# A two-layer hybrid backbone on one Trainium2 core: rooms for the two triangular solves, modulation weights by pairs, and other paces for the work run beside the matmuls

## The chip, the cores and the metric

The kernel runs on one core of a Trainium2 chip. The metric is the device time of one execution in microseconds (us); lower is better. Engines go by their names in the profile: PE is TensorE (matmuls and transposes; PEld its weight loads), DVE is VectorE, ACT is ScalarE, POOL is GpSimd, and SP issues most of the DMAs, from one queue in order. Each engine works through its own instructions in a fixed order and stops at the first one whose inputs are not there.

## The reference

The model has two layers on 256 latent tokens of width 2048, with 256 context tokens. Cut to what matters:

```python
# layer 0 (even): h = modulated latents, hc = modulated context
ka, va, kb, vb, a, b, qa, qb, za = split(h @ w_in)          # context: ka, va, kb, vb, a, b only
_, s_ctx = gdn_bidirectional(None, k_c, v_c, g_c, beta_c, zeros)   # recurrence over the context
o, _     = gdn_bidirectional(q, k, v, g, beta, s_ctx)              # recurrence over the latents
y_gdn = rmsnorm(o) * silu(za)
y_na  = neighbourhood_attention(qb, kb, vb, kb_ctx, vb_ctx, rpb)   # 8 heads
x = x + g1 * (concat(y_gdn, y_na) @ w_out)
x = x + g2 * swiglu(modulate(x, norm, sh2, sc2))
# layer 1 (odd): short convolution mixer, then the same kind of FFN
# per chunk of 64 tokens in gdn_bidirectional, for 8 heads and 2 directions:
t_inv = triangular_solve(eye + m, eye)     # m: 64 x 64, strictly lower
# and per layer: sh1, sc1, g1, sh2, sc2, g2 = split(silu(c) @ ada_w + ada_b)
```

All inputs are fp32.

## The kernel before, in words

**Matmuls.** Each product runs as three matmuls on values split into a high and a low part. A weight tile of 512 KB (`raw`) is loaded by SP, ScalarE copies its high part (`whi`, L176), VectorE subtracts to get the low part (`wlo`, L250), and TensorE multiplies with both. Three pairs of `whi`/`wlo` may stand ready at a time. TensorE needs a `wlo` from VectorE for every weight tile.

**Stages.** The input projection goes through its columns in the order KA, QA, VA (the recurrence's inputs), then KB and VB by halves (KB0, VB0, KB1, VB1: keys and values of the attention), QB0, QB1 (its queries) and ZA (the gate). The out projection follows in two halves (WO0, WO1), then the FFN of layer 0, and layer 1. Three kinds of side work run beside these stages, where the changed lines lie.

**1. The recurrence.** `chunk_matrices(1)` and `chunk_matrices(0)` prepare the context's and the latents' chunks: they build `nt` (the matrix m, L987), put aside its off-diagonal blocks (`n64`, `n32`), bring the 32 x 32 diagonal blocks into another layout by a store and eight gathers (`dl`, `lsol`), invert them in 31 pairs of VectorE instructions (L1029 product, L1031 subtract: "the solve") and store the result (`dz`). `inverses` joins blocks to 64 x 64 inverses, and `scan` goes over the chunks: each link is a fixed chain of matmul groups (L1123, L1132, L1143, L1165) with VectorE and ScalarE work between. `nt` and `lsol` share one room (tag "lsol"), and the context's `n64`/`n32` are written to DRAM (`nd64`, `nd32`) and read back. Which step of the stages calls which part is set by `plan`: `P_CH` for the latents' chunk, and the four numbers of `P_INV` for the inverses and scans; steps are counted from KB0 to QB1.

**2. The attention heads.** For each of eight heads `na_scores` loads a bias `bq` (L1307), adds a mask on VectorE (L1309), multiplies queries and keys (L1313, L1314) and takes the softmax (L1318 to L1322); `na_values` transposes and multiplies by the values (L1337).

**3. The modulation vectors of layer 0** (`ada_mixer`). Twelve blocks of 512 columns, each a sum over 16 weight tiles `araw` of 128 x 512: VectorE multiplies a tile by a scalar per partition and adds it to `acc` (L438). A block starts with a memset of `acc` (L430) and a DMA of its bias (L431), and closes with four matmuls (L445) that sum over partitions. `pump` takes a number of these steps per matmul step of the stage: `R_KB`, `R_QB`, `R_ZA` and `R_WO` are these paces. An L438 is tied behind the latest `wlo` at the place where it is written.

Within these bounds a scheduler at build time places the instructions of each engine.

At the hand-over from WO1 to the FFN a norm runs over the result: L1392 and L1393 add the projection to `xs`, L1411 scales a first half by the row norm (`rtmp`), L1447 the others (`xc`); TensorE transposes these, ScalarE modulates, and VectorE splits the FFN's inputs `fhi`, `flo` (L1459, L1465, L1466).

## Time and profile before

| | us |
|---|---|
| median of 3 runs | 2721.82 (2719.28 to 2724.71) |
| the profiled execution | 2726.88 |
| its span, first to last instruction | 2725.1 |
| TensorE busy in it | 2655.1 (97%) |
| VectorE busy in it | 1923.7 (71%) |
| ScalarE busy in it | 1279.2 (47%) |
| mean granted TensorE clock | 0.992 |

Durations and waits below come from the profiled execution. In its rows, "a <- b" says what an instruction writes and reads, or which releaser ended a wait; "x8" is a count. Where the stages lie in it, by TensorE's first and last matmul of each: KB0 from 337 us, VB0 from 387, KB1 from 438, VB1 from 493, QB0 and QB1 from 555 to 656, ZA from 661 to 738, the out projection from 743 to 874, and the FFN of layer 0 from 875. The context solve runs from 326 to 407 us, the latents' solve from 494 to 547.

### The profile page before, as it was taken

To read this page: it belongs to the slowest core of one execution; us is meant where nothing else is said; L and a number is where in the kernel's file an instruction comes from. 1 tells how busy PE (TensorE), PEld (TensorE's weight loads), DVE (VectorE), ACT (ScalarE), POOL (GpSimd) and SP (SyncE) were. 2 spreads that over 40 slices of the span, in tenths; PEclk is the share of its full clock that TensorE was granted. 3 is DMA by queue.
4 is the path that set the end of the run, shared out by engine and by line. 5 is a ranking of instruction groups with operands and counts; after the bars stand their busy time and mean duration, and the time that the engine had idled before them with its cause. 6 is when DMAs were issued, how large, how long until landed. Compare 5 with 4: busy or idle time off the path is not lost.

```text
span 2725.1 us, 37531 instructions
## 1 busy us (share of the span) xinstructions
PE 2655.1 (97%) x13775; PEld 2188.7 (80%) x13775; DVE 1923.7 (71%) x2652; ACT 1279.2 (47%) x1851; POOL 47.1 (2%) x73
## 2 busy tenths in 40 slices
...
GB/s 368 349 156 178 177 278 241 319 266 178 224 220 255 320 274 296 293 300 271 299 282 284 295 161 344 317 337 273 178 234 237 225 239 225 216 195 218 195 193 110
DMA packets 285124, 682.71 MB, mean 251 GB/s; under 512 B 56969, under 2 KB 98545, under 8 KB 283531
## 3 DMA queue, kind: packets, MB, share of 16 engines
...
q14 instruction: 77, 0.63, 0.1%
HBM read 658.16 MB, written 22.05 MB: 250 GB/s over the span
## 4 chain that ended last, share of the span: by engine, by line
PE 91%; DMA 3%; DVE 2%; ACT 2%; issue 1%; SPq 1%; DVEq 0%; ACTq 0%
PE mm L303 22%; PE mm L308 21%; PE mm L304 21%; PE mm L348 10%; PE mm L320 8%; PE sm L195 2%; PE sm L599 1%; PE gd L348 1%; DMA bq<-in_ev_rpb_dram 1%; DMA araw<-in_ada_w_dram 1%; PE sm L1337 1%; PE gd L1143 0%; PE gd L942 0%; DMA xn<-in_ctx_dram 0%; DVE wlo L250 0%
## 5 line engine op out<-in xcount | busy, mean ns | idle before, releaser
L250 DVE TENSOR_TENSOR wlo<-raw,whi 128x1024 fp32r<-128x1024 f32 x800 | 971.3, 1221 | 447.9 <-ACT whi L176 437.6
L176 ACT ACTIVATE whi<-raw 128x1024 fp32r<-128x1024 f32 x800 | 843.5, 1062 | 864.2 <-PE mm L308 636.2
L303 PE MATMUL mm<-whi,fhi 128*128 128x512 f32 x1232 | 482.3, 393 | 2.6 <-DVE fhi L1459 2.6
L304 PE MATMUL mm<-wlo,fhi 128*128 128x512 f32 x1232 | 479.8, 390 | 0.5 <-DVE wlo L250 0.5
L308 PE MATMUL mm<-whi,flo 128*128 128x512 f32 x1232 | 389.9, 390 | 0.0
L403 DVE SCALAR_TENSOR_TENSOR acc<-araw,cT,acc 128x1024 f32<-128x1024 f32 x224 | 286.5, 1279 | 37.6 <-DMA araw<-in_ada_w_dram 34.5
L303 PEld LDWEIGHTS mm<-whi,fhi 128*128 128x128 f32 x1232 | 231.6, 188 | 51.2 <-DVE fhi L1459 4.2
L308 PEld LDWEIGHTS mm<-whi,flo 128*128 128x128 f32 x1232 | 231.1, 188 | 48.4
L304 PEld LDWEIGHTS mm<-wlo,fhi 128*128 128x128 f32 x1232 | 231.5, 188 | 47.4 <-DVE wlo L250 0.9
L303 PE MATMUL mm<-whi,ahi 128*128 128x512 f32 x664 | 259.1, 390 | 0.0
L304 PE MATMUL mm<-wlo,ahi 128*128 128x512 f32 x664 | 258.3, 389 | 0.0
L348 PE MATMUL mm<-hB,whi 128*128 128x512 f32 (+1 forms) x840 | 235.3, 366 | 1.0 <-DVE hB L623 1.0
L308 PE MATMUL mm<-whi,alo 128*128 128x512 f32 x664 | 206.6, 389 | 0.0
L348 PEld LDWEIGHTS mm<-hB,whi 128*128 128x128 f32 x840 | 147.7, 189 | 24.3 <-DVE hB L623 2.2
L179 ACT ACTIVATE ahi<-prodT 128x256 fp32r<-128x256 f32 x176 | 73.1, 418 | 182.9 <-PE mm L304 178.1
L438 DVE SCALAR_TENSOR_TENSOR acc<-araw,cT,acc 128x512 f32<-128x512 f32 x192 | 142.4, 745 | 12.2 <-DMA araw<-in_ada_w_dram 10.9
L348 PE MATMUL mm<-hB,wlo 128*128 128x512 f32 (+1 forms) x420 | 149.5, 364 | 0.0
L308 PEld LDWEIGHTS mm<-whi,alo 128*128 128x128 f32 x664 | 124.6, 188 | 26.0
L303 PEld LDWEIGHTS mm<-whi,ahi 128*128 128x128 f32 x664 | 124.7, 188 | 25.7
L304 PEld LDWEIGHTS mm<-wlo,ahi 128*128 128x128 f32 x664 | 124.7, 188 | 25.5
L303 PE MATMUL mm<-whi,dhi 128*128 128x512 f32 x336 | 131.2, 393 | 1.2 <-DVE dhi L1459 1.2
L304 PE MATMUL mm<-wlo,dhi 128*128 128x512 f32 x336 | 130.8, 390 | 0.0
...
## 6 DMA issues: line engine op xcount, KB each, us to landing
...
raw<-in_ffn_w_down_dram SPq DMA_DIRECT2D x176, 512.0 KB
...
raw<-in_ev_w_in_dram SPq DMA_DIRECT2D x112, 512.0 KB
araw<-in_ada_w_dram SPq DMA_DIRECT2D x192, 256.0 KB
...
```

The lines of the kernel that those rows point to most:

```text
L176: ACT.activation(dst, src, AF.Copy)
L179: ACT.activation(hi, src, AF.Copy)
L195: return PE.transpose(dst, src, ident[:n, :n])
L250: last_lo[0] = DVE.tensor_tensor(lo, raw, hi, op=OP.subtract).ins
L303: PE.matmul(ps[ti][n], a, hi[:, n * 512:(n + 1) * 512], start=first, stop=False)
L304: ins = PE.matmul(ps[ti][n], a, lo[:, n * 512:(n + 1) * 512], start=False, stop=False).ins
L308: last_mm[0] = PE.matmul(ps[ti][n], b, hi[:, n * 512:(n + 1) * 512], start=False, stop=False).ins
L320: ins = PE.matmul(ps[ti][n], a(t), w[:, c_], start=False, stop=a is ll and hi is group[-1][0]).ins
L348: last_mm[0] = PE.matmul(o, wt, h_(slice(0, len(ws)), mv, k), start=i == 0 and g == 0 and j == 0, stop=i == len(ks) - 1 and g == len(group ...
L403: DVE.scalar_tensor_tensor(acc, raw, cT[:, k:k + 1], acc, op0=OP.mult, op1=OP.add)
L438: DVE.scalar_tensor_tensor(accs[n], raws.pop(i), cT[:, k:k + 1], accs[n], op0=OP.mult, op1=OP.add)
L599: ins = PE.matmul(pr[32 * j:32 * j + 32, :], cT2[:, g + j, :], raw[:, j].rearrange("p s n -> p (s n)"), start=g == 0, stop=g == KT - 4).ins
```

## The change

It has four parts.

- *Rooms.* The latents' chunk gets rooms of its own: `nt` and `lsol` lie in the two halves of `room`, the place that `state` takes later; `n32` and the solves' scratch lie in `half`. The context's off-diagonal blocks stay where they were built; the latents' `n32` alone goes through DRAM. Both quarters of the context's diagonal inverses are loaded at once.
- *Plan.* `P_CH` and the four numbers of `P_INV`.
- *Modulation weights.* One DMA brings two tiles (512 KB). The first tile of a block is a plain multiplication into `acc`, without memset and bias row; the bias is added to the closed sums as a column `bM`, which is transposed at the start together with the bias of the first two segments (`brow`, now 80 rows).
- *Paces.* `R_QB`, `R_KB`, `R_ZA`, `R_WO`.

```diff
@@ -41,16 +41,16 @@
 KH = 2
-P_CH = 2
-P_INV = (16, 22, 50, 56)
+P_CH = 1
+P_INV = (20, 26, 44, 50)
 AB = 6
...
 LATER = 2
-R_QB = 0.6
-R_KB = 1.6
-R_ZA = 2.0
-R_WO = 2.0
+R_QB = 1.5
+R_KB = 1.0
+R_ZA = 3.0
+R_WO = 1.6
 NST = 3
@@ -352,9 +352,14 @@
-    def ada_done(l, seg, kind, gamma, fs_, p):
-        if kind == "sc":
+    def ada_done(l, seg, kind, gamma, fs_, p, bias=None):
+        if bias is not None:
+            dst = scc[l, seg - 1] if kind == "sc" else (shc if kind == "sh" else gcol)[l, seg]
+            DVE.tensor_tensor(dst[:, fs_], p, bias, op=OP.add)
+            if kind == "sc":
+                DVE.scalar_tensor_tensor(dst[:, fs_], dst[:, fs_], 1.0, gamma[:, fs_], op0=OP.add, op1=OP.mult)
+        elif kind == "sc":
             DVE.scalar_tensor_tensor(scc[l, seg - 1][:, fs_], p, 1.0, gamma[:, fs_], op0=OP.add, op1=OP.mult)
@@ -426,16 +431,21 @@
             if not k:
-                acc = accs[n] = pool_.tile([128, 512], F32, name="acc", tag="acc", bufs=2)
-                DVE.memset(acc, 0.0)
-                SP.dma_start(acc[0:1, :], ada_b[0:1, c0:c0 + 512])
-            raws[i] = pool_.tile([128, 512], F32, name="araw", tag="araw", bufs=AB)
-            SP.dma_start(raws[i], wr[:, k, c0:c0 + 512])
+                accs[n] = pool_.tile([128, 512], F32, name="acc", tag="acc", bufs=2)
+            if k % 2:
+                return
+            raw = pool_.tile([128, 2, 512], F32, name="araw", tag="araw", bufs=AB // 2)
+            SP.dma_start(raw, wr[:, k:k + 2, c0:c0 + 512])
+            for j in range(2):
+                raws[i + j] = raw[:, j, :]
...
         def total(i):
...
             with tc.issue_after(last_lo[0]):
-                DVE.scalar_tensor_tensor(accs[n], raws.pop(i), cT[:, k:k + 1], accs[n], op0=OP.mult, op1=OP.add)
+                if k:
+                    DVE.scalar_tensor_tensor(accs[n], raws.pop(i), cT[:, k:k + 1], accs[n], op0=OP.mult, op1=OP.add)
+                else:
+                    DVE.tensor_scalar(accs[n], raws.pop(i), cT[:, 0:1], None, op0=OP.mult)
...
         def close(n):
@@ -443,11 +453,12 @@
                 PE.matmul(p[:, f:f + 1], acc[:, f * 128:(f + 1) * 128], ones[:, 0:1], start=True, stop=True)
-            ada_done(0, seg, kind, gamma, slice(b * 4, b * 4 + 4), p[:, 0:4])
+            m0 = (seg - 2) * 16 + b * 4
+            ada_done(0, seg, kind, gamma, slice(b * 4, b * 4 + 4), p[:, 0:4], bM[:, m0:m0 + 4])
             if kind == "row" and b == 3:
...
                 transpose(p[0:16, 0:128], gcol[0, seg])
-                g = pool_.tile([16, 128], F32, name="grow", tag="araw", bufs=AB)
+                g = pool_.tile([16, 128], F32, name="grow", tag="araw", bufs=AB // 2)
                 DVE.tensor_copy(g, p[0:16, 0:128])
@@ -457,7 +468,8 @@
                 total(i)
-                load(i + AHEAD)
+                if i:
+                    load(i + AHEAD - 2)
             if i >= KT + LAG - 1 and (i - LAG + 1) % KT == 0:
@@ -565,9 +577,9 @@
     ACT.dma_start(vrow[64:112, :], od_conv.rearrange("o t (k p) -> (o t k) p", p=128))
-    brow = sp.tile([32, 128], F32, name="brow")
+    brow = sp.tile([80, 128], F32, name="brow")
     bT = sp.tile([128, 32], F32, name="bT")
-    ACT.dma_start(brow, ada_b[0:1, 0:4096].rearrange("o (r p) -> (o r) p", p=128))
+    ACT.dma_start(brow, ada_b[0:1, 0:5 * D].rearrange("o (r p) -> (o r) p", p=128))
     ACT.dma_start(erow, ev_conv.rearrange("o t (k p) -> (o t k) p", p=128))
@@ -657,13 +669,15 @@
         p = smt()
-        transpose(p[:, 0:32], brow)
+        transpose(p[:, 0:80], brow)
         DVE.tensor_copy(bT, p[:, 0:32])
+        DVE.tensor_copy(bM, p[:, 32:80])
...
     gnb = epool.tile([128, 128], F32, name="gnb")
+    bM = epool.tile([128, 48], F32, name="bM")
@@ -871,7 +885,6 @@
     brest = epool.tile(gsh, F32, name="brest")
-    epool.tile([128, 48], F32, name="pad_e")
...
     def gates():
@@ -924,7 +937,8 @@
     flush()
-    state = gw.tile([128, 2, 8, 128], F32, name="state")
+    room = gw.tile([128, 2, 1024], F32, name="ntl", tag="state", bufs=1)
+    state = None
...
     def g4(name, tag, bufs=1):
@@ -954,6 +968,9 @@
+    half = []
+    nd32 = dram.tile([128, 16, 32], F32, name="nd32")
     def chunk_matrices(seq):
@@ -964,7 +981,7 @@
             n64 = lgo.tile([128, 1024], F32, name="n64", tag="o_t", bufs=2).rearrange("p (n c) -> p n c", n=16)
-            n32 = g4("n32", "vtok")[:, 0:512].rearrange("p (n c) -> p n c", n=16)
+            n32 = half[0][:, 0:512].rearrange("p (n c) -> p n c", n=16)
             dgs = lgo.tile([128, 1024], F32, name="dgs", tag="o_t", bufs=2)
@@ -977,7 +994,8 @@
                 tok = slice(ti * 128, ti * 128 + 128)
-                nt = gw.tile([128, 2, 4, 128], F32, name="nt", tag="lsol", bufs=1)
+                nt = (gw.tile([128, 2, 4, 128], F32, name="nt", tag="lsol", bufs=1) if seq else
+                      room[:, 0, :].rearrange("p (d i e) -> p d i e", d=2, i=4))
                 ems = [decay(d, t0 + ti, q) for d in range(2)]
@@ -1007,11 +1025,12 @@
-        lsol = g4("lsol", "lsol").rearrange("p (r c) -> p r c", r=32)
-        nd64 = dram.tile([128, 16, 64], F32, name="nd64", tag="nd64", bufs=2)
-        nd32 = dram.tile([128, 16, 32], F32, name="nd32", tag="nd32", bufs=2)
-        SP.dma_start(nd64, n64)
-        SP.dma_start(nd32, n32)
+        lsol = (g4("lsol", "lsol") if seq else room[:, 1, :]).rearrange("p (r c) -> p r c", r=32)
+        if seq:
+            half.append(g4("half", "vtok"))
+        else:
+            SP.dma_start(nd32, n32)
+            n32 = None
         dl = dram.tile([4, 32, 32, 32], F32, name="dl", tag="dl", bufs=2)
@@ -1022,7 +1041,7 @@
         POOL.memset(zsol.rearrange("p r c -> p (r c)")[:, ::33], 1.0)
-        sub_tmp = g2("sub_tmp").rearrange("p i e -> p (i e)")
+        sub_tmp = half[0][:, 512 + seq * 256:768 + seq * 256]
         for j in range(31):
@@ -1036,14 +1055,12 @@
                 SP.dma_start(dz[v, :, :, d].rearrange("b q t e -> (b q) t e"), src)
-        return nd64, nd32, dz
-    def load_offdiag(parts):
-        n64 = gw.tile([128, 16, 64], F32, name="n64", tag="n64", bufs=1)
+        return n64, n32, dz
+    def own_offdiag(n64):
         n32 = gw.tile([128, 16, 32], F32, name="n32", tag="n32", bufs=1)
-        SP.dma_start(n64, parts[0])
-        SP.dma_start(n32, parts[1])
+        SP.dma_start(n32, nd32)
         return n64, n32
...
     def load_diag(dz, q, tag="diag"):
@@ -1213,22 +1230,21 @@
     def own_chunks():
...
         own = chunk_matrices(0)
-        off = load_offdiag(parts)
-        diag = load_diag(parts[2], 0)
+        off = parts[:2]
+        diag = [load_diag(parts[2], q, ("diag", "kT")[q]) for q in range(2)]
...
     def first_inverse():
-        nonlocal diag
-        xdTs.append(inverses(off, diag, 0))
-        diag = load_diag(parts[2], 1)
+        xdTs.append(inverses(off, diag[0], 0))
...
     def second_inverse():
-        nonlocal off, diag
-        xdTs.append(inverses(off, diag, 1))
+        nonlocal off, diag, state
+        xdTs.append(inverses(off, diag[1], 1))
+        state = gw.tile([128, 2, 8, 128], F32, name="state", tag="state", bufs=1)
         for q in range(2):
...
         xdTs.clear()
-        off = load_offdiag(own)
-        diag = [load_diag(own[2], q, ("diag", "kT")[q]) for q in range(2)]
+        off = own_offdiag(own[0])
+        diag = [load_diag(own[2], q, ("diag", "n64")[q]) for q in range(2)]
...
     def first_own():
...
```

In the changed file L438 has become L446 (and L448 for a block's first tile), L445 L455, L984 to L1005 stand 18 lines lower (L987 is L1005), L1029 and L1031 are L1048 and L1050, the scan's groups stand 17 lines lower (L1123 is L1140, L1165 is L1182), and the heads and the norm 16 lines (L1313 is L1329, L1337 is L1353, L1411 is L1427, L1447 is L1463).

How the instructions move shows at three places. VectorE around the end of the context solve, before (L1032 copies the solve's result; L996 and L997 belong to the latents' chunk, and none of its rows of L987 stands above these):

```order
L1031 TENSOR_TENSOR zsol<-zsol,sub_tmp 128x2x30
L1029 TENSOR_TENSOR sub_tmp<-lsol,zsol 128x31
L1031 TENSOR_TENSOR zsol<-zsol,sub_tmp 128x31
L250 TENSOR_TENSOR wlo<-raw,whi 128x1024
L1032 COPY lsol<-zsol 128x1024
L438 SCALAR_TENSOR_TENSOR acc<-araw,cT,acc 128x512 x2
...
L987 SCALAR_TENSOR_TENSOR nt<-gd,beta,em 128x128 x8
L996 TENSOR_TENSOR em<-em,cs 128x512
L1002 STREAM_TRANSPOSE dgs<-nt 32x128 x4
```

and now, where `ntl` is the latents' `nt` and `half` the scratch:

```order
L1050 TENSOR_TENSOR zsol<-zsol,half 128x10x22
L1005 SCALAR_TENSOR_TENSOR ntl<-gd,beta,em 128x128 x3
L1048 TENSOR_TENSOR half<-lsol,zsol 128x207
L1005 SCALAR_TENSOR_TENSOR ntl<-gd,beta,em 128x128 x5
...
L1048 TENSOR_TENSOR half<-lsol,zsol 128x31
L1005 SCALAR_TENSOR_TENSOR ntl<-gd,beta,em 128x128 x8
...
L1051 COPY lsol<-zsol 128x1024
L1015 TENSOR_TENSOR AT<-gd,em 128x512 x2
...
L1005 SCALAR_TENSOR_TENSOR ntl<-gd,beta,em 128x128 x8
...
L1048 TENSOR_TENSOR half<-ntl,dgs 128x31
L1050 TENSOR_TENSOR dgs<-dgs,half 128x31
```

Three of the four groups of eight `ntl` rows stand inside the context solve, and the latents' solve (the last two rows) begins some 20 rows after the context's last link.

TensorE where the latents' scan ends and the out projection nears, before (L303 to L308 and L320 are the big matmuls; L195 are transposes, here of the softmax `s` and of `o_t`):

```order
L308 MATMUL mm<-whi,ylo 128x512 x2
L1123 MATMUL gd<-state,kT 128x128 x4
L1132 MATMUL gd<-state,qT 128x128 x4
L1143 MATMUL gd<-R,xdT 128x128 x4
L1165 MATMUL gd<-vn,AT 128x128 x4
...
L1313 MATMUL gd<-kb,qb 128x512
L1314 MATMUL gd<-bq,cs 128x256
...
L195 MATMUL gd<-cs,s 128x128 x4
L195 MATMUL sm<-cs,s 128x128 x4
L1337 MATMUL gd<-PT,vb 128x256 x4
...
L1337 MATMUL sm<-PT,vb 128x256 x4
```

and now, at the last two heads:

```order
L308 MATMUL mm<-whi,hC 128x512 x2
...
L1329 MATMUL gd<-kb,qb 128x512
L1330 MATMUL gd<-bq,cs 128x256
L1329 MATMUL sm<-kb,qb 128x512
L1330 MATMUL sm<-bq,cs 128x256
L303 MATMUL mm<-whi,hC 128x512
L304 MATMUL mm<-wlo,hC 128x512
...
L195 MATMUL gd<-cs,s 128x128 x4
L303 MATMUL mm<-whi,hC 128x512
L195 MATMUL sm<-cs,s 128x128 x4
...
L1353 MATMUL gd<-PT,vb 128x256 x4
```

The scan's links ended earlier, and groups of ZA's big matmuls (`hC`) stand between the heads' groups.

VectorE in the norm at the hand-over from WO1 to the FFN, before:

```order
L438 SCALAR_TENSOR_TENSOR acc<-araw,cT,acc 128x512
L223 SCALAR_TENSOR_TENSOR nx0s<-nx0s,nx0v 128x1
L224 SCALAR_TENSOR_TENSOR nx0r<-nx0s,nx0r 128x1
L1411 TENSOR_SCALAR rtmp<-xs,nx0r 128x512
L1392 TENSOR_TENSOR rtmp<-mm,row 128x512
L1393 TENSOR_TENSOR xs<-rtmp,xs 128x512
L358 SCALAR_TENSOR_TENSOR sc_84<-sm,vecT 128x4
L1459 CAST fhi<-modt 128x128 x4
...
L250 TENSOR_TENSOR wlo<-raw,whi 128x1024
...
L1447 TENSOR_SCALAR xc<-xs,nx1r 128x512
```

and now:

```order
L446 SCALAR_TENSOR_TENSOR acc<-araw,cT,acc 128x512
L1427 TENSOR_SCALAR rtmp<-xs,nx0r 128x512
L1408 TENSOR_TENSOR rtmp<-mm,row 128x512
L446 SCALAR_TENSOR_TENSOR acc<-araw,cT,acc 128x512
L1409 TENSOR_TENSOR xs<-rtmp,xs 128x512
L446 SCALAR_TENSOR_TENSOR acc<-araw,cT,acc 128x512 x3
L1475 CAST fhi<-modt 128x128 x2
...
L446 SCALAR_TENSOR_TENSOR acc<-araw,cT,acc 128x512 x2
L1418 TENSOR_REDUCE ss_7475<-ssx 128x1
...
L1463 TENSOR_SCALAR xc<-xs,nx1r 128x512
```

The products of the last modulation block (L446), which closed ahead of the norm before, stand between the norm's instructions, 12 of them between L1427 and the first L1463, and a first tile and three more (not shown) just ahead of L1427, where two stood before.

## The prediction, made before the changed kernel ran

> **What bounds the kernel now.** I read the page's engine totals and chain first, then the busy time by stretch, then the waits of TensorE and of VectorE in the stretches where TensorE loses time.
>
> ```profile
> span 2725.1 us, 37531 instructions
> ...
> PE 2655.1 (97%) x13775; PEld 2188.7 (80%) x13775; DVE 1923.7 (71%) x2652; ACT 1279.2 (47%) x1851; POOL 47.1 (2%) x73
> ...
> PE 91%; DMA 3%; DVE 2%; ACT 2%; issue 1%; SPq 1%; DVEq 0%; ACTq 0%
> ```
>
> TensorE is busy for 97% of the span. The change removes no matmul, so it can only win time in which TensorE stands, or runs at a lower clock. 2725.1 − 2655.1 = 70 us is idle. The stretches that hold the edited work:
>
> ```profile
> core 0: us, PE busy (x) PEld busy (x) DVE busy (x) ACT busy (x) POOL busy (x), PEclk, DMA share, GB/s
> 430.00:440.00 10.00, 8.91 (x48) 7.64 (x47) 9.47 (x21) 4.02 (x9) 1.61 (x4) 0.94 1.01 368
> 440.00:490.00 50.00, 50.00 (x316) 42.28 (x315) 38.68 (x72) 15.04 (x27) 4.21 (x10) 0.98 0.71 233
> 490.00:510.00 20.00, 18.72 (x236) 14.80 (x236) 16.49 (x37) 5.88 (x9) 0.95 (x1) 1.00 0.94 312
> 560.00:590.00 30.00, 23.76 (x173) 23.36 (x172) 14.98 (x27) 8.44 (x14) 1.81 (x1) 0.89 0.80 218
> 620.00:660.00 40.00, 34.93 (x656) 30.20 (x643) 21.64 (x41) 17.98 (x35) 0.00 (x0) 0.96 0.66 183
> 730.00:790.00 60.00, 51.15 (x286) 42.92 (x285) 37.75 (x92) 38.51 (x100) 0.00 (x0) 0.94 0.43 147
> 860.00:890.00 30.00, 25.56 (x117) 20.70 (x115) 23.22 (x52) 13.40 (x31) 0.00 (x0) 0.89 0.39 131
> ```
>
> The first number after the comma is TensorE's busy time, and PEclk its granted clock. Idle time plus (1 − clock) × length gives what each stretch loses: 430–490: 1.09 + 0.6 + 1.0 = 2.7 us; 490–510: 1.3; 560–590: 6.2 + 3.3 = 9.5; 620–660: 5.1 + 1.6 = 6.7; 730–790: 8.9 + 3.6 = 12.5; 860–890: 4.4 + 3.3 = 7.7. In all that is 40 us. No edit reaches the rest of the idle time but by a trifle at the head. The low clock stands behind an idle stretch each time; it is a cost of the stall.
>
> TensorE's waits name the causes (engine, line, whom it waited for, total, times, longest):
>
> ```profile
> PE mm L348 <- DVE wlo L250: 4.4, 1, 4.4
> ...
> PE sm L1337 <- DVE PT L173: 4.4, 2, 3.7
> PE gd L1143 <- DMA vtok<-vd__151: 1.9, 1, 1.9
> ...
> PE gd L1337 <- ACT PT L171: 3.7, 1, 3.7
> PE gd L1123 <- DVE state L1156: 1.5, 1, 1.5
> PE sm L195 <- DVE s L1322: 1.5, 1, 1.5
> PE gd L1165 <- DVE o_t L1137: 1.1, 1, 1.1
> ...
> PE sm L445 <- DVE acc L438: 3.2, 1, 3.2
> ```
>
> The first three lie in 560–660, the next four in 730–790, the last at the hand-over from the out projection to the first FFN. VectorE's own waits, of 320–440 and of 560–680:
>
> ```profile
> DVE sub_tmp L1029 <- DMA lsol<-dl: 4.6, 1, 4.6
> DVE nt L987 <- DMA dz<-lsol: 4.4, 1, 4.4
> ...
> DVE bq L1309 <- DMA bq<-in_ev_rpb_dram: 32.5, 8, 7.4
> ```
>
> VectorE works in order. A wait for a bias tile bq holds every wlo behind it, and TensorE needs a wlo for each weight tile. One stall traced whole:
>
> ```profile
> 570.01 0.56 DVE L1309 TENSOR_TENSOR bq<-bq,cs 128x384 f32<-128x384 f32 x1 [7.33 <-DMA bq<-in_ev_rpb_dram]
> 570.48 1.22 DVE L250 TENSOR_TENSOR wlo<-raw,whi 128x1024 fp32r<-128x1024 f32 x1
> ...
> 571.76 0.39 PE L348 MATMUL mm<-hC,wlo 128*128 128x256 f32 x1 [4.36 <-DVE wlo L250]
> ```
>
> **The change, part by part.**
>
> *Own rooms for the latent solve.* The latent chunk's nt no longer waits for the context solve's stores: 4.4 us of VectorE. The order shows the whole latent chunk pulled ahead: three of its four groups of L1005 stand inside the context solve (before, all came after it), and its solve starts some 20 VectorE rows after the context's. The gathers of lsol still stand ahead of it, so I keep one wait like the 4.6 us there. TensorE lost 2.7 us in 430–490, and the nt wait is the cause of its 1.09. I take a gain of 1.7, from 0 (the gathers' wait takes its place) to 2.7. 490–510 I leave as it is.
>
> The gain proper comes later. In the order of after, the latent scan's links lie 10 to 20 big matmuls apart from QB0 to ZA, and heads 6 and 7 of the attention lie inside ZA. Before, two whole links (L1123 to L1165) and both heads stood on TensorE with no big matmul between. A link or head waits for an answer from VectorE or ScalarE; the four waits of 730–790 (1.1 to 3.7 us) are these answers. A group of six big matmuls lasts 1.4 us, by the spacing of 0.23 that eight of them show in a row:
>
> ```profile
> 863.82 0.39 PE L320 MATMUL mm<-wlo,yhi 128*128 128x512 f32 x1
> ...
> 865.41 0.39 PE L320 MATMUL mm<-whi,ylo 128*128 128x512 f32 x1
> ```
>
> so two groups cover an answer of 2.8 us, and ten to twenty matmuls (2.3 to 4.6 us) nearly all. Of the 12.5 us I leave 2 for the o_t transposes still next to WO0: gain 10.5, from 5 (a head's answer of 3.7 us outlasts its cover, and the clock drops once) to 12.5.
>
> *QB0 and QB1.* The three bq loads that cost 7.3, 4.0 and 2.7 us at 570–586 now stand close together behind one weight load, so one wait of 7 stays in place of 14. With more link work in QB0, TensorE takes about a third longer for each tile, so three split tiles cover more. Of 9.5 us I take 4.5 as gained (0 to 8). In 620–660 the 3.7 us wait is a head's answer, which now has matmuls behind it: 3.5 of 6.7 gained (0 to 5.5).
>
> *Paces.* The same 192 multiply-adds are pumped elsewhere. Prices:
>
> ```profile
> L438 DVE SCALAR_TENSOR_TENSOR acc<-araw,cT,acc 128x512 f32<-128x512 f32 x192 | 142.4, 745 | 12.2 <-DMA araw<-in_ada_w_dram 10.9
> L250 DVE TENSOR_TENSOR wlo<-raw,whi 128x1024 fp32r<-128x1024 f32 x112 | 135.4, 1218 | 32.7 <-ACT whi L176 32.2
> L430 DVE MEMSET acc<- 128x512 f32 x10 | 4.8, 485 | 0.6
> ...
> 590.00:730.00 140.00, 134.93 (x1278) 116.93 (x1277) 93.97 (x176) 61.35 (x130) 2.76 (x2) 0.99 0.73 220
> ...
>   DVE acc L438: 10.9, 13
> ```
>
> Between the wlo's of QB1 and the end of ZA the order counts 45 multiply-adds in place of 34: 11 × 0.745 = 8.2 us. With the heads and links that moved in, the operations at their own rows' durations add about 20 us. VectorE was busy for 94 us of the 140 in 590–730, and waited there for most of the later bq loads. 94 + 20 = 114, plus some 18 of bq waits, is 132 of 140: it fits, with hardly any slack, and VectorE's order is fixed. Late wlo's could cost TensorE 0 to 16 us (two or three stalls as that of 4.4, each with 1.6 us of low clock). I take 4, nearest to the single stall on record.
>
> The other move is at the hand-over. The last ada block of 16 now runs inside the norm chain: 12 multiply-adds between L1427 and the first xc (L1463), none there before, and four instead of two just ahead of L1427. That chain in before:
>
> ```profile
> 869.28 0.49 DVE L1411 TENSOR_SCALAR rtmp<-xs,nx0r 128x512 f32<-128x512 f32 x1
> ...
> 874.52 0.63 DVE L1459 CAST fhi<-modt 128x128 fp32r<-128x128 f32 x4 [3.36 <-PE mm L320]
> ...
> 879.39 0.49 DVE L1447 TENSOR_SCALAR xc<-xs,nx1r 128x512 f32<-128x512 f32 x1
> ...
> 880.82 0.60 PE L195 MATMUL sm<-cs,xc 128*128 128x128 f32 x4
> ...
> 882.23 0.50 PE L303 MATMUL mm<-whi,fhi 128*128 128x512 f32 x1 [0.81 <-DVE fhi L1459]
> ```
>
> 14 instructions more at 0.66 us (0.745 less the 0.09 by which an instruction starts before the one ahead ends, as 570.01 + 0.56 and 570.48 show) are 9.2 us, of which the idle 3.36 us takes 3.4: xc comes about 6 us later, and TensorE, which has only the first 24 FFN matmuls ahead of it, stands for it. The 3.2 us wait for the closing L445 goes, since the block now closes behind those matmuls; but rtmp, next in line, comes 1.3 us later than before, so half of that wait stays. I take a loss of 7: 6 + 1.3 for the two delays, less 1.8 of the old wait, and 1.5 us more at the low clock; from 2 (cover by the next weight tiles) to 11 (both stalls, full low clock).
>
> A rule bears on that. The Trainium skill, "TensorE: Matmul & The Clock Gate", section "HAM oscillation — how this bites in real kernels", says that a wait which crosses the activity window drops TensorE to the half clock, and that the next work starts cold. The stretches above agree (0.89 in 860–890 beside 3.2 us of waiting); by the rule alone a 6 us wait would always bring a cold restart, and the hand-over would cost 8 rather than 7.
>
> *Paired loads and the bias column.* SP issues 96 araw and 12 bias loads fewer, at 0.33 us each by the row below; nothing on TensorE's path waits for them. Twelve memsets (12 × 0.485 = 5.8 us) go; the first product becomes a tensor_scalar (0.49 us for the same size, by the xc row) in place of a multiply-add. That relieves VectorE by 9 us over 700, hidden behind TensorE, and is in the balance above. Against it, pairs mean 3 rooms of two in place of 6, so a load can wait for two products. The 10.9 us that VectorE waited for araw may go or double; I count it at 0, ±1. At the head brow brings 80 rows in place of 32 ahead of erow on ScalarE's queue:
>
> ```profile
> L433 SPq DMA_DIRECT2D araw<-in_ada_w_dram x192: 327/328/2325, 140.2 to 860.6; - x192
> ...
> PE sm L195 <- DMA erow<-in_ev_conv_dram: 5.9, 1, 5.9
> ...
> L570 ACTq DMA_DIRECT2D brow<-in_ada_b_dram x1: 368/368/368, 3.0 to 3.0; - x1
> ```
>
> TensorE waits 5.9 us for erow; one more load as brow would be 0.4 us. I take 0.3 lost (0 to 0.5).
>
> **Sum.** 1.7 + 10.5 + 4.5 + 3.5 − 4 − 7 − 0.3 = 8.9 us gained. The profiled execution took 2726.88, 1.8 above its span and 5 above the median; it would come to 2718. By the median of the runs, 2721.82 − 8.9 = 2712.9.
>
> **Rivals.** *No change.* The heads' answers outlast their cover (10.5 becomes 6), VectorE costs 7, the hand-over 7, QB0/QB1 give 6: 1.7 + 6 + 6 − 7 − 7 − 0.3 = −0.6, about 2722. For it speaks that the two losses are in the order itself; against it, that 730–790 is the largest and its cause is plainly moved.
>
> *Slower: VectorE becomes the bound in QB1 and ZA.* The multiply-adds that R_QB 1.5 puts into QB1 share VectorE with bq waits, and in-order wlo's come late. It decides once VectorE's work and waits in 590–730 exceed TensorE's 140 us, so if the bq waits there stay above 26 instead of my 18 (32.5 stood in 560–680). Price 16, and QB0/QB1 give only 3 as the same waits bite there: 1.7 + 10.5 + 3 − 16 − 7 − 0.3 = −8, about 2730.
>
> *A larger gain.* The hand-over costs 2, since the next weight tiles stand ready, and VectorE 0: 1.7 + 12.5 + 6 + 4 − 2 − 0.3 = 22, about 2700. For it: three split tiles were full before 730; against it: the norm chain feeds all FFN matmuls.
>
> *The solves don't run at once.* The order shows the context solve's last link before the latent solve's first. Only the chunk overlaps; had the links not moved with it, gains of 1.7 and the losses would be left, 2731. The links did move, so I fold its small chance into the slower case.
>
> **Numbers.** Forecast (2706 to 2717) 0.38; no change 0.22; slower 0.20; larger gain 0.20. A difference of 0.2% (5.4 us) is about what a measurement of this kernel can tell from none. So faster 0.38 + 0.20 = 0.58, same 0.22, slower 0.20. The bounds summed would reach from 2695 to 2735; leaving out a tenth at each end gives 2700 to 2729. The likeliest case's own range is 2706 to 2717.
>
> **What would show it.** Right: no wait above 2 us on TensorE where ZA passes to WO0, L1353 there without a 3.7 us wait; a clock of 1.00 over it; the wait of L1005 for dz gone; at the hand-over a wait of 5 us or more for xc or fhi with L446 rows ahead of it on VectorE. Wrong: TensorE waits on wlo L250 of several us in QB1 and ZA with bq rows ahead (the slower case); no wait at the hand-over (the larger gain); bq waits above 30 us in all. If the context and latent links stand next to each other again, the first term was misread.

## The result, and the profile after

The changed kernel takes 2738.95 us, median of 4 runs (2734.23 to 2739.94), beside 2722.59 for the kernel before in the same comparison. The ratio is 1.0057, 95% interval 1.0042 to 1.0072: slower by 16 us, where 9 us of gain were forecast, and outside the range. The profiled execution took 2739.08 us, so it stands for the median; that of before took 2726.88, some 4 above its own.

The page of the changed kernel, first the totals and then the chain of work that ended last:

```profile
span 2737.3 us, 37225 instructions
...
PE 2656.9 (97%) x13775; PEld 2189.4 (80%) x13775; DVE 1918.1 (70%) x2645; ACT 1282.1 (47%) x1852; POOL 49.9 (2%) x73
...
PE 83%; DMA 7%; DVE 6%; ACT 1%; issue 1%; SPq 1%; POOL 0%; DVEq 0%; ACTq 0%
```

TensorE works as long as before (2655.1) on as many matmuls, and VectorE 5.6 us less. What grew is idle time, 70.0 to 80.4 us, and time at a low clock. TensorE's share of the chain fell from 91% to 83%; DMA and VectorE took it.

Busy time by stretch in the changed kernel (columns as in the prediction: length, TensorE busy, ..., PEclk). The stretches are KB1, QB, ZA, the 40 us from ZA's end, and the hand-over (14 us before the last matmul of the out projection to 26 us behind it); the same five in the kernel before follow:

```profile
447.00:511.00 64.00, 57.66 (x437) 47.19 (x436) 43.37 (x86) 16.82 (x28) 0.95 (x1) 0.95 0.72 220
568.00:686.00 118.00, 104.80 (x1194) 95.58 (x1193) 83.59 (x160) 46.66 (x105) 0.00 (x0) 0.96 0.81 246
686.00:768.00 82.00, 80.43 (x419) 66.31 (x417) 53.70 (x108) 43.90 (x103) 0.00 (x0) 1.00 0.45 135
768.00:808.00 40.00, 34.01 (x145) 27.11 (x144) 34.42 (x54) 18.22 (x20) 0.00 (x0) 0.87 1.02 405
864.00:904.00 40.00, 30.79 (x135) 24.55 (x134) 33.53 (x70) 15.70 (x32) 0.00 (x0) 0.83 0.56 172
```

```profile
436.00:493.00 57.00, 55.91 (x344) 47.27 (x344) 44.76 (x85) 19.18 (x36) 5.82 (x14) 0.97 0.72 235
555.00:656.00 101.00, 90.72 (x1072) 83.04 (x1073) 57.20 (x106) 41.82 (x85) 4.58 (x3) 0.95 0.79 229
656.00:738.00 82.00, 80.97 (x470) 69.22 (x467) 55.27 (x102) 35.82 (x80) 0.00 (x0) 1.00 0.62 193
738.00:778.00 40.00, 31.23 (x187) 25.84 (x186) 30.14 (x69) 28.08 (x76) 0.00 (x0) 0.99 0.58 197
860.00:900.00 40.00, 35.56 (x162) 28.97 (x161) 33.11 (x64) 23.40 (x51) 0.00 (x0) 0.91 0.46 153
```

Idle time plus (1 − clock) × length, as in the prediction, gives the loss of each stage; the last column is the forecast gain worked out there. PEclk has two digits, so a long stretch is good to half a us.

| stage | before | after | change | forecast |
|---|---|---|---|---|
| KB1 | 1.1 + 1.7 = 2.8 | 6.3 + 3.2 = 9.5 | 6.7 lost | 1.7 gained |
| QB | 10.3 + 5.1 = 15.4 | 13.2 + 4.7 = 17.9 | 2.5 lost | 8.0 gained |
| ZA | 1.0 | 1.6 | 0.6 lost | 4 lost |
| ZA's end | 8.8 + 0.4 = 9.2 | 6.0 + 5.2 = 11.2 | 2.0 lost | 10.5 gained |
| hand-over | 4.4 + 3.6 = 8.0 | 9.2 + 6.8 = 16.0 | 8.0 lost | 7 lost |

These make 19.8 us. VB1 gives 1.3 back, the rest of the out projection 2.5, and what follows takes 1.2 more: 17 in all. The spans of these two executions differ by less, 12.2 us (idle time 10.4 more, busy time 1.8), and the medians by 16.4. The sum is too high in part because idle time at a low clock counts twice in it (2.0 us of that at the hand-over, below). So the losses show where time goes, and do not add up to the kernel's time to better than some 5 us. Of the two losses that were forecast for these stages, the hand-over's came at its size and ZA's hardly; the three gains did not come at all.

TensorE's waits in these stretches of the changed kernel, KB1 first, then QB, ZA's end and the hand-over:

```profile
PE gd L1160 <- DMA vtok<-vd__152: 3.6, 1, 3.6
PE mm L348 <- DVE nst L173: 2.7, 2, 2.1
...
PE sm L1353 <- DVE PT L173: 4.6, 2, 2.3
PE sm L195 <- ACT s L1336: 2.4, 1, 2.4
PE gd L1109 <- issue: 1.8, 1, 1.8
...
PE mm L303 <- ACT whi L176: 4.8, 2, 2.6
PE mm L304 <- DVE wlo L250: 1.2, 1, 1.2
...
PE sm L195 <- DVE rtmp L1427: 4.3, 1, 4.3
PE sm L455 <- DVE acc L446: 2.6, 1, 2.6
PE mm L303 <- DVE fhi L1475: 1.7, 2, 0.9
```

**KB1.** The wait of nt for the solve's stores is gone, and so is TensorE's wait for nt. In its place the context scan, whose matmuls on vtok begin some 48 us earlier than before (490.1 and 538.1 us), waits for vtok. SP's queue and TensorE there:

```profile
477.59 1.22 SPq L1057 DMA_DIRECT2D dz<-dgs  x2
478.94 2.89 SPq L1057 DMA_DIRECT2D dz<-ntl  x2
481.88 1.23 SPq L963 DMA_DIRECT2D vtok<-vd__152  x1
...
490.06 2.05 PE L1160 MATMUL gd<-vtok,xdT 128*128 128x128 f32 x8 [3.60 <-DMA vtok<-vd__152]
```

`half`, the scratch of both solves, lies in the place of vtok. The latents' solve uses it to its last subtraction, at 477.0 us; then SP issues the four stores of the solve, and only then the load of vtok, which arrives 8 us later. The diff says so (`g4("half", "vtok")`). The 2.7 us of waits for nst, the copies of the stage's results, make up the rest of the 6.3 us idle here; what delays them was not traced.

**ZA's end.** The heads' answers are indeed covered: no wait for them is left there. But the out projection's first weights come late. SP's queue:

```profile
741.95 0.53 SPq L1344 DMA_DIRECT2D vb<-vb_d  x1
765.46 0.38 SPq L438 DMA_DIRECT2D araw<-in_ada_w_dram  x1
765.93 1.86 SPq L236 DMA_DIRECT2D raw<-in_ev_w_out_dram  x2
```

and what held it from 742 to 765 (SP's waits from 718 to 798 us: line, whom it waited for, total, times, longest):

```profile
SPq L438 <- DVE acc L446: 28.0, 6, 23.0
```

A load of modulation weights stood at the head of the queue for 23.0 us until a product (L446) freed its room, and the loads of the out projection stood behind it. TensorE ended ZA at 768.1; the first of these loads had been issued 2.2 us earlier.

**Hand-over.** VectorE's and TensorE's rows:

```profile
874.00 0.48 DVE L1427 TENSOR_SCALAR rtmp<-xs,nx0r 128x512 f32<-128x512 f32 x1
...
877.41 1.54 DVE L446 SCALAR_TENSOR_TENSOR acc<-araw,cT,acc 128x512 f32<-128x512 f32 x2 [0.40 <-DMA araw<-in_ada_w_dram]
...
888.72 0.49 DVE L1463 TENSOR_SCALAR xc<-xs,nx1r 128x512 f32<-128x512 f32 x1
```

```profile
874.63 1.09 PE L195 MATMUL sm<-cs,rtmp 128*128 128x128 f32 x4 [4.34 <-DVE rtmp L1427]
...
888.40 1.67 PE L455 MATMUL sm<-cs,acc 128*128 128x1 f32 x8 [2.64 <-DVE acc L446]
```

From rtmp to xc VectorE takes 14.7 us, where it took 10.1 (869.28 to 879.39): the products in between. TensorE stands for rtmp, and then at the closing sum (L455), just ahead of xc's transposes. Behind each of the two waits its clock is at half:

```profile
871.59:878.41 6.82, 3.65 (x10) 2.58 (x10) 6.39 (x15) 1.97 (x6) 0.00 (x0) 0.50 0.78 235
888.65:895.48 6.83, 6.02 (x21) 4.84 (x21) 5.93 (x14) 3.39 (x6) 0.00 (x0) 0.50 0.00 0
```

In these 13.7 us TensorE is idle for 4.0, half of which the loss of 16.0 counts twice; counted once it is 14.0.

### The profile page after: what moved, and what is told of

Same layout as the page of the kernel before. It is cut to its first block, busy times and chain, and to the rows that moved or that the text cites. A ratio compares the mean times of both kernels' runs of the same rounds, so it can differ in the third digit from the quotient of the medians.

```text
span 2737.3 us, 37225 instructions
## 1 busy us (share of the span) xinstructions
PE 2656.9 (97%) x13775; PEld 2189.4 (80%) x13775; DVE 1918.1 (70%) x2645; ACT 1282.1 (47%) x1852; POOL 49.9 (2%) x73
## 4 chain that ended last, share of the span: by engine, by line
PE 83%; DMA 7%; DVE 6%; ACT 1%; issue 1%; SPq 1%; POOL 0%; DVEq 0%; ACTq 0%
PE mm L303 20%; PE mm L304 20%; PE mm L308 20%; PE mm L348 9%; PE mm L320 7%; DMA araw<-in_ada_w_dram 3%; PE sm L195 2%; DVE wlo L250 1%; DMA bq<-in_ev_rpb_dram 1%; DVE acc L446 1%; PE sm L611 1%; PE gd L348 1%; DVE acc L408 1%; PE gd L956 1%; DMA raw<-in_ev_w_out_dram 1%
## 5 line engine op out<-in xcount | busy, mean ns | idle before, releaser
L303 PE MATMUL mm<-whi,fhi 128*128 128x512 f32 x1232 | 483.0, 394 | 3.0 <-DVE fhi L1475 3.0
L308 PE MATMUL mm<-whi,flo 128*128 128x512 f32 x1232 | 390.1, 390 | 0.0
L303 PEld LDWEIGHTS mm<-whi,fhi 128*128 128x128 f32 x1232 | 232.0, 188 | 51.9 <-DVE fhi L1475 4.8
L308 PEld LDWEIGHTS mm<-whi,flo 128*128 128x128 f32 x1232 | 231.1, 188 | 48.4
L303 PE MATMUL mm<-whi,ahi 128*128 128x512 f32 x664 | 259.0, 390 | 0.0
L308 PE MATMUL mm<-whi,alo 128*128 128x512 f32 x664 | 206.5, 389 | 0.0
L308 PEld LDWEIGHTS mm<-whi,alo 128*128 128x128 f32 x664 | 124.6, 188 | 25.9
L303 PEld LDWEIGHTS mm<-whi,ahi 128*128 128x128 f32 x664 | 124.6, 188 | 25.8
L446 DVE SCALAR_TENSOR_TENSOR acc<-araw,cT,acc 128x512 f32<-128x512 f32 x180 | 134.5, 747 | 9.8 <-DMA araw<-in_ada_w_dram 8.2
L303 PE MATMUL mm<-whi,dhi 128*128 128x512 f32 x336 | 131.1, 393 | 2.3 <-DVE u_t L1630 1.2
```

The costliest lines, as they stand in the source:

```text
L303: PE.matmul(ps[ti][n], a, hi[:, n * 512:(n + 1) * 512], start=first, stop=False)
L308: last_mm[0] = PE.matmul(ps[ti][n], b, hi[:, n * 512:(n + 1) * 512], start=False, stop=False).ins
L446: DVE.scalar_tensor_tensor(accs[n], raws.pop(i), cT[:, k:k + 1], accs[n], op0=OP.mult, op1=OP.add)
```

## The experiments

The theory after reading the trace: the paces decide. R_KB 1.0 takes products out of KB and VB, where VectorE has slack (busy 29 of the 60 us from 500 to 560 in the changed kernel), and leaves a backlog that stands in the norm at the hand-over and, on SP's queue, ahead of the out projection's weights. Rivals: the rooms, whose sharing holds up the context scan; and the paired loads, whose three rooms hold SP's queue.

Each kernel below was compared with the kernel before on the same chip. The losses are worked out as in the table above, from each kernel's profiled execution. That took from 8 us less (new rooms with R_KB 2.0; 6 less with the other scratch) to 5 us more than the kernel's median, so differences of a few us between the rows' losses need not stand in the medians. "Products" are those of the modulation blocks, counted between the wlo's of a stage in the kernel's order.

| kernel | median us | ratio to before (95%) | KB1 | VB1 | QB | ZA's end | hand-over |
|---|---|---|---|---|---|---|---|
| changed kernel | 2738.95 | 1.0057 (1.0042–1.0072) | 9.5 | 0 | 17.9 | 11.2 | 16.0 |
| changed, old paces | 2724.75 | 1.0014 (1.0004–1.0023) | 11.9 | 2.9 | 8.6 | 9.4 | 9.6 |
| before, new paces | 2734.72 | 1.0049 (1.0032–1.0066) | 6.7 | 0 | 17.7 | 11.2 | 20.5 |
| before, new rooms | 2721.75 | 1.0003 (0.9993–1.0013) | 8.0 | 1.5 | 7.9 | 9.1 | 9.0 |
| changed, single loads | 2743.66 | 1.0086 (1.0071–1.0101) | 5.6 | 0 | 18.0 | 1.6 | 25.8 |
| changed, R_KB 1.6 | 2726.12 | 1.0014 (1.0004–1.0025) | 11.8 | 4.8 | 17.8 | 8.1 | 1.5 |
| changed, R_KB 1.3 | 2724.44 | 1.0011 (1.0002–1.0021) | 9.2 | 0 | 17.7 | 6.9 | 1.4 |
| changed, late products left out | 2723.32 | 1.0003 (0.9994–1.0013) | 6.5 | 0 | 15.2 | 10.6 | 1.5 |
| changed, R_QB 0.6 | 2750.03 | 1.0097 (1.0079–1.0115) | 10.0 | 0 | 20.7 | 11.0 | 19.8, and 11 behind |
| changed, old paces, other scratch | 2729.37 | 1.0023 (1.0010–1.0036) | 8.6 | 2.2 | 14.9 | 0.8 | 8.5 |
| before, pairs | 2732.80 | 1.0038 (1.0023–1.0053) | 0 | 6.4 | 28.9 | 10.5 | 4.2 |
| before, new rooms and plan | 2721.59 | 0.9999 (0.9990–1.0008) | 11.6 | 1.0 | 8.9 | 11.3 | 6.5 |
| before, new rooms, R_KB 2.0 | 2736.20 | 1.0050 (1.0035–1.0065) | 9.4 | 14.5 | 5.7 | 10.6 | 1.4 |
| changed, old paces, R_KB 2.0 | 2738.69 | 1.0060 (1.0039–1.0081) | 15.9 | 9.8 | 9.0 | 15.9 | 1.4 |
| before, new rooms, R_QB 1.0 | 2718.22 | 0.9984 (0.9974–0.9994) | 12.1 | 1.0 | 14.9 | 8.6 | 1.5 |
| changed, single loads, R_KB 1.6 | 2724.58 | 1.0008 (0.9998–1.0017) | 9.8 | 2.4 | 15.0 | 9.1 | 1.5 |
| changed, loads from GpSimd | 2761.66 | 1.0150 (1.0129–1.0171) | 13.8 | 0 | 33.3 | 4.7 | 32.2 |
| the same, R_KB 1.3 | 2732.52 | 1.0039 (1.0020–1.0058) | 1.4 | 0 | 23.5 | 8.5 | 1.4 |

**Which of the three parts.** One part undone, or one part alone:

```diff
 # old paces (changed kernel), and the reverse in the kernel before
-R_QB, R_KB, R_ZA, R_WO = 1.5, 1.0, 3.0, 1.6
+R_QB, R_KB, R_ZA, R_WO = 0.6, 1.6, 2.0, 2.0
 # new rooms alone: only the hunks on room, half, nd32 and the diagonals
 # single loads: the modulation hunks of the diff taken back
```

> The changed kernel with the four old paces back (R_QB 0.6, R_KB 1.6, R_ZA 2, R_WO 2); rooms, plan and paired loads stay. Its order has no modulation product behind L1427 any more (the changed kernel has 12). If the paces are the cause (they take products out of KB and VB, where VectorE has slack, and leave a backlog that ends in the norm at the hand-over and ahead of the out projection's weight loads), it comes down by 14 to 22 us from 2739, to 2717 to 2725, and the stall at the hand-over falls from 16 us (idle and low clock in 860-900) to the 8 of before or less. If the rooms are the cause (the context scan's vtok and the evacuations of VB0 wait behind the latents' solve), it stays at 2731 or more, since that part is unchanged. If the paired loads are the cause, it stays at 2735 or more.

> The kernel before with the four new paces alone. If the paces are the cause: slower than before by 8 to 18 us (2731 to 2741), with a hand-over as in the changed kernel (15 products stand behind the norm's first scaling in its order). If rooms or paired loads are the cause: within 4 us of before.

> The kernel before with the new rooms alone (old plan, old paces, single loads). If the paces are the cause of the whole loss: within 5 us of before, to the faster side (2717 to 2723), since the latents' chunk no longer waits for the stores. If the rooms are the cause (scratch of both solves in the place of vtok until the latents' solve has ended): slower by 6 to 12 us (2729 to 2735), with waits of TensorE on vtok and nst in 440-500.

> The changed kernel with single modulation loads, memsets and bias rows back; rooms, plan and new paces stay. If pairs are the cause (three rooms of two tiles hold SP's queue ahead of the out projection's weights): faster than 2739 by 8 us or more. If the paces are the cause: no faster, rather slower by 2 to 8 us (2739 to 2747), since 26 products instead of 12 stand behind the norm's first scaling.

The old paces bring the changed kernel from 1.0057 to 1.0014; the new paces alone cost the kernel before 1.0049. The rooms alone cost nothing that can be told. Single loads make it worse, as there are then 26 products in the norm instead of 12 (hand-over 25.8). So the paces are the main cause, and neither rooms nor pairs are. The table shows where: the hand-over and QB. The parts do not simply add up, though. With new paces and single loads, the rooms and their plan cost something after all (1.0086 beside 1.0049): there are 26 products in the norm instead of 15. And KB1's loss rises with the rooms alone (8.0, from 2.8) as well as with the paces alone (6.7). One expectation missed: the old paces brought the hand-over to 9.6, not to 8 or less.

**Which pace.** R_KB and R_QB undone singly, in the changed kernel:

```diff
-R_KB = 1.0
+R_KB = 1.6        # after_kb16
-R_QB = 1.5
+R_QB = 0.6        # after_qb06
```

> The changed kernel with R_KB back at 1.6 alone; R_QB 1.5, R_ZA 3 and R_WO 1.6 stay. In its order KB0 to VB1 hold 92 products instead of 58, and none stands behind the norm's first scaling. If the low R_KB is the cause (products taken out of stages with slack come back as a backlog at the hand-over), the hand-over falls from 16 us to 8 or less and the time to 2722 to 2731. If the high R_QB is the cause (25 products in QB1 beside the waits for bq), the time stays at 2733 or more, with QB's loss at 17.

> The changed kernel with R_QB back at 0.6 alone. 17 instead of 44 products stand in QB, but 29 instead of 12 behind the norm's first scaling. If the low R_KB with its backlog is the cause: no faster than 2736, up to 2748, QB's loss falling from 18 to 9 and the hand-over's rising from 16 to 20 or more. If the high R_QB is the cause: 2722 to 2730.

R_KB alone takes back as much as all four paces together (1.0014 both). With R_QB back at 0.6 instead, 29 products stand behind the norm's first scaling and the kernel is slower still, by 11 us, 2 beyond the expected range. TensorE's waits there, in that kernel:

```profile
PE sm L455 <- DVE acc L446: 14.8, 2, 10.0
PE sm L195 <- DVE rtmp L1427: 2.0, 1, 2.0
```

So the high R_QB is not the cause; it works against the backlog. QB's loss was expected to fall to 9 with only 17 products there, and this missed: it is 20.7, with a wait of 7.3 us for the result of a closing sum among TensorE's waits. The number of products in QB does not set QB's loss by itself.

**Is it the late products themselves?** Undoing a pace moves products through all stages. The first of the next two kernels keeps every pace and the order up to WO1; it leaves out 14 of 16 tiles in the last two modulation blocks, and so part of the modulation: some 21 us of VectorE's work (28 x 0.745) and 14 loads. The second leaves nothing out and takes a step between.

```diff
         def total(i):
             n, k = divmod(i, KT)
+            if n >= len(blocks) - 2 and k > 1:
+                return
 # and the same bound in load(i); after_kb13 has only:
-R_KB = 1.0
+R_KB = 1.3
```

> The changed kernel with all its paces, but the last two of the twelve modulation blocks multiply only 2 of their 16 tiles (28 products and 14 loads left out). Its order up to WO1 is that of the changed kernel, and no product stands behind the last wlo of WO1. If the late products themselves cost the hand-over: its loss falls from 16 us to 3 or less and the time from 2739 to 2723 to 2729, the other stages as they are. If the low pace of KB costs by what it does before (QB, ZA): 2733 or more.

> The changed kernel with R_KB 1.3, between its 1.0 (2739) and the old 1.6 (2726). 75 products in KB0 to VB1, 45 in QB, and none behind the last wlo of WO1. If the late products are what 1.0 costs: already 2723 to 2729 here, with 4 us or less lost at the hand-over. If the cost goes with the number of products moved out of KB to VB1: about half way, 2731 to 2735.

Both come out as expected if the late products are the cost. The hand-over's row in the kernel without the late products, and in that with R_KB 1.3 (beside 30.79 busy of 40 at 0.83 in the changed kernel):

```profile
853.00:893.00 40.00, 38.55 (x184) 31.14 (x183) 32.13 (x60) 25.82 (x54) 0.00 (x0) 1.00 0.48 149
```

```profile
857.00:897.00 40.00, 38.61 (x187) 31.29 (x186) 31.73 (x61) 24.88 (x52) 0.00 (x0) 1.00 0.47 146
```

Without its late products the changed kernel comes down by 15.6 us. The hand-over's loss falls by 14.5 (12.5 with idle time counted once), KB1's and QB's by 3 each, and ZA's end stays nearly as it was. And 0.3 of pace, which closes the last block in time, does the same as 0.6: the cost hangs on whether the last block closes ahead of the norm, not on how many products were moved. The kernel before lost 8 us here too, with two products and a closing sum just ahead of its norm's first scaling; a clean hand-over loses 1.5.

**Is it SP's queue that ate the gain at ZA's end?** The modulation loads leave SP's queue:

```diff
-            SP.dma_start(raw, wr[:, k:k + 2, c0:c0 + 512])
+            POOL.dma_start(raw, wr[:, k:k + 2, c0:c0 + 512])
 # after_kb13_pool also: R_KB = 1.3
```

> The changed kernel with the paired modulation loads issued by GpSimd instead of SP, so that a load that waits for its room no longer stands ahead of the out projection's weights on SP's queue. 19 products instead of 12 stand behind the norm's first scaling. If SP's queue is what ate the gain at ZA's end: no wait there for whi behind a late weight load, that stage's loss falls from 11 us to 5 or less, while the hand-over's stays at 16 or grows to 22; 2733 to 2742 in all. If the weights are late for another reason (the DMA engines, or the rooms of the weights themselves): the loss at ZA's end stays at 9 or more.

> The same with R_KB 1.3, where the last block closes ahead of the norm. If queue and late products were the two costs of the changed kernel: 2714 to 2722, faster than with R_KB 1.3 alone (2724.4), with a clean hand-over (1.5) and 5 us or less lost at ZA's end (6.9 without). If issue from GpSimd has a cost of its own (slower landing, VectorE held): 2725 or more.

At ZA's end, yes: the loss falls from 11.2 to 4.7, TensorE's waits for whi (4.8) and wlo (1.2) are gone, and this is all that is left of waits there:

```profile
PE gd L195 <- DVE o_t L1218: 1.1, 1, 1.1
...
781.00:821.00 40.00, 38.88 (x173) 32.11 (x172) 34.79 (x55) 20.58 (x24) 5.08 (x7) 0.91 0.97 374
```

So part of the gain that was forecast there existed (4.5 us of 10.5, from the 9.2 of before), and the load at the head of SP's queue held it. A second kernel agrees: in the changed kernel with single loads, a modulation load waits there for its room for 2.1 us at most, and ZA's end loses 1.6. But this is not the only way to lose time there. In the changed kernel with the old paces a wait of 5.0 us for whi stands there, though no modulation load waits longer than 2.8 us for its room; in the kernel before with the new paces it is a head's softmax, 6.5 us.

As a kernel the one with loads from GpSimd is worse by far: 2761.66, well above what was expected. The hand-over loses 32.2 with 19 late products, and QB 33.3 in place of 17.9. With R_KB 1.3 the hand-over is clean, but the time is 2732.52, not 2714 to 2722: ZA's end is no better than without (8.5 and 6.9; with SP's queue a modulation load waited there for its room for 1.9 us at most, so there was nothing to take away), and VB0 loses 15.2 where it lost 1.4. GpSimd also zeroes the rooms of the solve and of the diagonals, and its queue is in order too. What its loads of modulation weights stood idle for in the first of these kernels, two of the rows (releaser, total, times):

```profile
  DVE acc L446: 286.9, 52
...
  DVE half L1048: 53.6, 7
```

That the zeroing behind such waits is what costs QB and VB0 is likely, but was not taken apart.

**The paired loads.** Alone in the kernel before, beside the single loads in two others:

```diff
 # before, pairs: the modulation hunks of the diff alone, with brow, bM and pad_e
 # before, new rooms and plan: the room hunks, P_CH = 1, P_INV = (20, 26, 44, 50)
 # changed, single loads, R_KB 1.6: the modulation hunks taken back, R_KB = 1.6
```

> The kernel before with the paired loads and the bias column alone (old rooms, plan and paces). If pairs relieve VectorE and SP as counted and hold nothing up: within 4 us of before, rather faster (2717 to 2722). If three rooms of two tiles hold SP's queue: slower by 4 us or more, with longer waits of VectorE for araw or of ScalarE for raw.

> The kernel before with the new rooms and the new plan; single loads and old paces. Beside the changed kernel with old paces (2724.75) it lacks the paired loads alone. If pairs cost time with these rooms as they did with the old ones (10 us): 2715 to 2722. If pairs cost nothing here and the rooms with their plan make the 4 us left: 2723 to 2727.

> The changed kernel with R_KB 1.6 and single loads (memset and bias row back); rooms, plan and the other new paces stay. If pairs are what keeps the changed kernel with R_KB 1.6 at 2726: 2715 to 2722. If pairs cost nothing here: 2724 to 2729.

In the old rooms pairs cost 1.0038, with QB's loss at 28.9 in place of 15.4. With the new rooms and the old paces the ratio goes from 0.9999 to 1.0014 by them, some 4 us; the intervals (up to 1.0008, and from 1.0004) overlap, so this is likely and no more. With the new paces and R_KB 1.6 it is 1.0008 against 1.0014, which tells nothing. So pairs never helped except by shortening the backlog (2743.66 to 2738.95). How they cost time in QB isn't settled. VectorE's waits for bq were as long as before there (31.7 and 32.5 us); TensorE's longest waits there are for the scan's state (7.0) and for vtok (4.1).

**The place of vtok.** The latents' solve gets scratch as before the change, so that vtok's place is free ahead of that solve:

```diff
-        sub_tmp = half[0][:, 512 + seq * 256:768 + seq * 256]
+        sub_tmp = half[0][:, 768:1024] if seq else g2("sub_tmp").rearrange("p i e -> p (i e)")
```

> The changed kernel with the old paces, and the scratch of the latents' solve in a room of the rotating kind, as before the change, instead of in the place of vtok; vtok's place is then free once the latents' n32 is stored, ahead of that solve. If the wait for vtok in KB1 (3.6 us and the low clock behind it; KB1 loses 12 us in this kernel's parent) comes from that shared place: KB1's loss falls by 4 us or more and the time to 2716 to 2721. If the order of SP's queue or the state's place holds vtok's user anyway: within 3 us of its parent's 2724.75.

Half of the expectation holds. SP's first load of vtok, in the kernel with old paces and in this one:

```profile
502.69 2.20 SPq L963 DMA_DIRECT2D vtok<-vd__152  x1
```

```profile
440.61 0.49 SPq L963 DMA_DIRECT2D vtok<-vd__152  x1
```

The load is issued 62 us earlier, so the shared place does hold it back. TensorE's wait for vtok is gone, but with the old paces that was 0.9 us, not the 3.6 of the changed kernel, so what those are worth was not tried. KB1's loss falls by 3.3 us, less than the 4 expected, and the time does not fall (2729.37 beside 2724.75): QB loses 14.9 in place of 8.6.

**More pace in KB, and a better kernel.** If the backlog is the trouble, a higher R_KB or R_QB should close the block early:

```diff
-R_KB = 1.6
+R_KB = 2.0        # rooms_kb20 and oldpace_kb20
-R_QB = 0.6
+R_QB = 1.0        # rooms_qb10
```

> The kernel before with the new rooms and R_KB at 2.0 in place of 1.6 (single loads, old plan, other paces old). KB0 to VB1 hold 116 products in its order instead of 99, WO1 8 instead of 28, and none stands behind the last wlo of WO1. If the pace of KB decides by what it leaves for the hand-over: faster than the rooms alone (2721.75) by 5 to 9 us, so 2712 to 2717, with 3 us or less lost at the hand-over in place of 9. If VectorE is short in VB1 already (43 products there beside 13 links of the solve): 2722 or more, with late wlo's or evacuations in VB1.

> The changed kernel with R_KB 2.0 and the other three paces old. 101 products in KB0 to VB1, 34 in QB, 4 in WO1. By the backlog theory: the hand-over loses 3 us or less in place of 9.6, and the time falls from 2724.75 to 2716 to 2721. If the loads by pairs hold it back (the loss in KB1 and QB): 2723 or more.

> The kernel before with the new rooms and R_QB at 1.0 in place of 0.6. 33 products instead of 21 stand in QB, and the last block closes in WO1. If products in QB beside the waits for bq cost little and an early close helps: 2713 to 2719, the hand-over's loss falling from 9 to 3. If they starve TensorE in QB: 2723 or more, QB's loss rising from 8 to 14 or more.

R_KB 2.0 cleans the hand-over (1.4 in both) and loses more than that elsewhere: with the rooms alone 13.0 more in VB1, in the changed kernel with old paces 6.9 more in VB1, 6.5 at ZA's end and 4.0 in KB1. Both are 14 to 16 us slower than before, where the backlog theory gave 2712 to 2721. In the first of the two (its profiled execution took 2728.30 us, below its median), TensorE's and VectorE's longest waits from 500 to 580 us, which hold VB1:

```profile
PE gd L1147 <- DVE R L1130: 7.9, 1, 7.9
```

```profile
DVE acc L438 <- DMA araw<-in_ada_w_dram: 21.9, 7, 8.8
```

VectorE stood up to 8.8 us at a product whose weights had not arrived, and the scan's R stood behind such products. The slack of VB1 in VectorE's busy time can't be filled at will: VectorE works in order, and the products come no faster than their loads.

R_QB 1.0 with the rooms alone is the one kernel that beats the kernel before: 2718.22 us, ratio 0.9984 (0.9974 to 0.9994), 4 us. Its hand-over is clean. QB loses 14.9 in place of the 7.9 of the rooms alone, as the rival expected, but the hand-over gives back more.

## Why the prediction was wrong, by its own steps

- **What bounds the kernel: right.** TensorE's work did not change (2655.1 and 2656.9 us); what grew in the profiled executions is 10.4 us of idle time and, behind the stalls, time at a low clock.
- **Own rooms, 1.7 gained in KB1: wrong, 6.7 lost.** The wait that it named went. The step looked at VectorE's waits alone, and did not ask what had lain in the places that `half` and `room` take: the context scan, which runs earlier now, needs vtok's place, and had to wait 3.6 us for a load that stood behind the latents' solve. That is about half of KB1's idle time; the waits for nst (2.7) are the rest, and the loss of 6.7 in the paces' kernel with the old rooms shows that the rooms are not its only source. The second wait that it kept, ahead of the latents' solve, is there on VectorE, 7.2 us where it took 4.6.
- **Links and heads among big matmuls, 10.5 gained at ZA's end: wrong, 2.0 lost.** The order was read rightly and the answers are covered. The step costed TensorE's rows and left SP's queue out: a modulation load 23.0 us at its head, the next stage's weights behind it. It said of SP's modulation loads that "nothing on TensorE's path waits for them"; the loads behind them on the queue do, and off that queue the stage's loss is 4.7. The sign that it named, no wait above 2 us there and a clock of 1.00, did not show: 2.6 us for whi, and 0.87.
- **QB, 8.0 gained: wrong, 2.5 lost.** TensorE's wait for wlo (4.4) is gone, as forecast. Waits for the heads (PT 4.6, s 2.4) and for links took its place, so the head's answer of 3.7 us, whose cover was to give 3.5, was not covered here. The bq waits came to 20.2 us in QB and 25.4 in all, close to what was assumed (7 and 18). That a gain was there shows in the rooms alone, where QB loses 7.9; the new paces took it (17.7 in the kernel before with the paces alone).
- **Late wlo's, 4 lost in QB1 and ZA: wrong in kind.** TensorE has no wait for a wlo there. The rival built on it (VectorE the bound through R_QB 1.5) had the right sign and a time of 2730, but the wrong cause: with R_QB 0.6 the kernel is slower.
- **Hand-over, 7 lost: right, 8.0** (some 6 with idle time counted once), by the mechanism described and shown by leaving the products out. The size is in part luck: xc came 4.6 us later behind rtmp, not 6; the wait for rtmp was 4.3 us where 1.4 was left for it; and the closing sum, whose wait was to go, held TensorE for 2.6 us ahead of xc, where a wait of 5 us for xc was named as the sign. What the prediction missed is where it came from: it speaks of R_QB's effect on VectorE and takes the late block as given, where R_KB 1.0 made it, with half of VectorE free in VB1.
- **Head, 0.3 lost: right in sum,** 26.3 and 26.6 us idle in the first 300 us, though erow's wait grew from 5.9 to 7.2 us; the wait for xn behind it shrank (6.9 to 6.1).
- **Low clock.** TensorE's clock is at half behind the hand-over's wait of 4.3 us, and again behind that of 2.6 (PEclk 0.83 over the 40 us; 4.8 us of the loss with idle time counted once). A rule of the Trainium skill ("TensorE: Matmul & The Clock Gate", "HAM oscillation — how this bites in real kernels") would have a long wait at the hand-over bring a cold restart; the trace agrees.

In sum, 20.2 us of gains were booked from TensorE's and VectorE's rows; in each of the three places something that these rows don't show (a shared place, SP's queue, the next answer in line) ended the wait later.

Open remains by which path pairs cost QB 13 us in the old rooms, and why QB's loss stays at 18 to 21 us when either R_KB or R_QB alone is put back, where both together bring it to 8.6 (TensorE's longest waits differ: 7.3 us for a closing sum's result with R_QB 0.6, 3.7 for a head's PT with R_KB 1.6). Open is also what the shared place of vtok costs in the changed kernel itself.
